# Triangular inverses for two head pairs at once, decays by one masked scan, and a new order of the mixers' parts

## The chip, the cores and the metric

The kernel runs on one core of one Trainium2 chip. The metric is the device time of one execution in microseconds; the time before is the median of three runs. The core has TensorE (matrix products, written to PSUM), VectorE, ScalarE and GpSimd (POOL) for elementwise work, and SyncE (SP), which here only issues transfers; ScalarE and POOL issue some too. Each engine takes its instructions in the order in which the program holds them.

## What is computed

The reference is one layer of a hybrid decoder on 512 tokens of width 1024, in float32: RMS norm, one wide input projection, four token mixers of width 512, gates that merge them, then a gated feed-forward part with a short convolution, a gated per-layer input, and a last norm.

```python
h = rmsnorm(x, norm_mix); proj = h @ w_in
xa, xb, xc, xd, g = split(proj)
branches = (pool_mixer(xa), rwkv7_mixer(xb), spatial_gating_mixer(xc), hgrn2_mixer(xd))
merged = sum(sigmoid(g[k]) * (branches[k] @ w_branch[k]) for k in range(4))
x = x + merged @ w_out
x = x + conv_glu_ffn(rmsnorm(x, norm_ffn))
x = x + (p @ ple_proj) * sigmoid(rmsnorm(x, norm_ple) @ ple_gate)
return rmsnorm(x, norm_final)
```

The change is in the second mixer. It has 8 heads of width 64 and a state that is decayed and corrected at every token:

```python
w = -softplus(-(w0 + tanh(lw) @ w2)) - 0.5;  decay = exp(-exp(w))
sa = einsum('bhvk,bhk->bhv', state, -kk_t)
state = state * w_t + sa[..., None] * (kk_t * a_t) + v_t[..., None] * k_t
y_t = einsum('bhvk,bhk->bhv', state, r_t)
```

## The kernel before

Activations lie with channels on the 128 partitions and the 512 tokens along the free axis, eight tiles for the width of 1024. A float32 product is made of three faster ones: each operand is split into a rounded part hi and a remainder lo (`split`, L76: a cast on ScalarE, L77, and a difference on VectorE or POOL, L78), and `mm3` (L118) issues hi*hi, hi*lo and lo*hi (L119 to L121). A weight block of 128 x 1024 (512 KB) is loaded by SP into one of two raw buffers and split into a ring of four (NWS) hi and four lo tiles, tags wh and wl; a block of 256 output columns and eight input tiles takes two places in each ring. The gemms write into four PSUM banks (`mm_ps`), all other products into four more (`sm_ps`).

The second mixer works on four head pairs j, each two heads of 64 channels, and on eight chunks of 64 tokens:

- `rwkv_proj` (task x): three projections r, k, v of a pair. `rwkv_decay` (w): decay and step size; the sigmoid and an Exp give the decay per token (L382 to L385).
- `rwkv_prep` (prep): E, the running product of the decays inside each chunk, by eight scans on VectorE (L399); the normed key kk; its head sums by a product with a block mask (pk, pb); 1/E by a reciprocal (L422); the factors ard, BK and BD; and v turned (pv into M).
- `rwkv_forms` (forms): products of these per chunk (pg, L471), masked into AR (L475), and written to DRAM, from which the strictly triangular 32 x 32 blocks come back into U with one block on each of 32 partitions.
- `rwkv_inverse` (inv): 30 steps of elimination on U, two VectorE instructions each (L496, L498), a write to DRAM, and eight block loads into two zeroed tiles TB, issued by ScalarE's and SP's queues. Then the off-diagonal blocks: transposes Ts (L518), products pW (L521) and pT (L527) with evictions, and copies on ScalarE that refill AR (L534) once pW has read it.
- `rwkv_chain` (chain j.half): eight dependent steps per pair, each three products (cx, cu, cs) with small evictions between (L550, L554, L563).
- `rwkv_finish` (fin) reads the outputs, norms them, and stores them; `rwkv_out` brings all four back.

The other tasks are the pool (pool), the spatial gating (sgp, sgv, sgn, sgu), the gated recurrence (masks, hv, hg, head, ho), and per branch and column block `gates` (gate) and `merge`. A gate's sigmoid (L880) goes straight from PSUM on ScalarE; the branch product is multiplied into it on VectorE.

The order is written out by hand in ORDER: the tasks are emitted as they stand there, those with "!" with an earlier due time. A planner then orders each engine's instructions when the program is built, by due time among those that its own cost model says are ready; on the chip each engine keeps to that order. Buffers of one tag are a ring: a tile that has no free place makes its first writer wait.

After the mixers come the output projection, the feed-forward part (its activated tiles, tag act, in 44 places) and the ple stage, in which four gate weights (wpg) pass through the same ring of split weights.

Of the kernel before, what the change touches and what calls it, by code (L numbers as in the profile page):

```python
# [16 lines left out]
P = 128  # L17
# [13 lines left out]
NR, NF, NWR, NWS, NA = 22, 7, 2, 4, 4  # L31
# [17 lines left out]
def hybrid_kernel(ctx, tc, x, p, norm_mix, w_in, pool_w, pool_scale, rwkv_mu, rwkv_w0, rwkv_w2, rwkv_a0,  # L49
# [65 lines left out]
    def wcols(w, c0, name, early=True):  # L115
        return wload(w[:, c0:c0 + WB].rearrange("(k p) c -> p k c", p=P), KD, WB, name, early)
# [160 lines left out]
    zer = cp.tile([P, C], F32, name="zer")  # L277
    G.memset(zer, 0.0)
# [15 lines left out]
    low, oml, noml = lbs[:, 3], lbs[:, 4], lbs[:, 5]  # L294

# [77 lines left out]
    def rwkv_decay(j):  # L373
        assert "lora" in ready
        pt = sm_ps(f"pw{j}")
        pa = sm_ps(f"pa{j}")
        js = slice(j * P, (j + 1) * P)
        for i, o in enumerate((pt, pa)):
            PE.matmul(o, lwa[i][:, js], mwa[i], start=True, stop=False)
            PE.matmul(o, lwa[i][LH[i], js], mlo[LH[i], :], start=False, stop=True)  # L380
        wd = rt(f"wd{j}")
        S.activation(wd, pt, AF.Sigmoid, bias=ctab["w0"][:, j:j + 1])  # L382
        a = rt(f"a{j}")
        S.activation(a, pa, AF.Sigmoid, bias=ctab["a0"][:, j:j + 1])
        S.activation(wd, wd, AF.Exp, scale=-math.exp(-0.5))  # L385
        rw[j].update(wd=wd, a=a)
# [6 lines left out]
    def rwkv_prep(j):  # L393
        js = slice(j, j + 1)
        r, k, v, wd, a = (rw[j].pop(n) for n in (0, 1, 2, "wd", "a"))
        E = rt(f"E{j}")
        for c in range(NCH):
            cs = slice(c * C, (c + 1) * C)
            V.tensor_tensor_scan(E[:, cs], wd[:, cs], zer, 1.0, ALU.mult, ALU.add)  # L399
# [21 lines left out]
        Em = nr  # L421
        V.reciprocal(Em, E)  # L422
# [37 lines left out]
    def rwkv_forms(j):  # L460
# [23 lines left out]
        U = rg.tile([32, 32, 32], F32, tag="U", name=f"U{j}")  # L484
        sf = scr1.rearrange("(f s) (c g t) -> f c s g t", f=2, g=2, t=32)
        for f in range(2):
            (nc.scalar, nc.sync)[f].dma_start(U[f * 16:(f + 1) * 16], sf[f, :, :, f, :])
        rw[j].update(AR=AR, BKe=BKe, U=U)

    def rwkv_inverse(j):  # L490
        U, AR, ard = (rw[j][n] for n in ("U", "AR", "ard"))
        tmp = rg.tile([32, 16 * 16], F32, tag="Ut", name=f"Ut{j}")
# [8 lines left out]
        scr2 = dp.tile([32, 1024], F32, tag="scr2", name=f"scr2_{j}")  # L501
        nc.scalar.dma_start(scr2, Uf)
        s2 = scr2.rearrange("(f i c h) (s t) -> f i h s c t", f=2, i=2, h=2, s=32)
# [3 lines left out]
        Ts = Ws = rg.tile([P, 2, HC, 32], F32, tag="Ts", name=f"Ts{j}")  # L507
        for i in range(2):
            G.memset(TB[i], 0.0)
            for h in range(2):  # L510
                for f in range(2):
                    (nc.scalar, nc.sync)[f].dma_start(TB[i][(lo, hi)[f][h], :, h, f * 32:f * 32 + 32], s2[f, i, h])

        blocks = lambda q: q[:, :T // 2].rearrange("p (i c x) -> p i c x", i=2, c=HC)
        pw, pt = ([blocks(sm_ps(f"p{n}{j}_{h}")) for h in range(2)] for n in "WT")
        for h in range(2):
            for i in range(2):
                V.transpose(Ts[lo[h], i], TB[i][lo[h], :, h, 0:32])  # L518
                for c in range(HC):
                    q = i * HC + c  # L520
                    PE.matmul(pw[h][hi[h], i, c, :], AR[q // 2][lo[h], q % 2, 0, h, 32:C], Ts[lo[h], i, c, :],  # L521
                              start=True, stop=True, tile_position=(lo[h].start, hi[h].start))
            V.tensor_copy(Ws[hi[h]], pw[h][hi[h]])
        for h in range(2):
            for i in range(2):
                for c in range(HC):
                    PE.matmul(pt[h][lo[h], i, c, :], Ws[hi[h], i, c, :], TB[i][hi[h], c, h, 32:],  # L527
                              start=True, stop=True, tile_position=(hi[h].start, lo[h].start))
                V.tensor_copy(TB[i][lo[h], :, h, 32:], pt[h][lo[h], i])

        for q in range(4):
            cs = slice(q % 2 * 2, q % 2 * 2 + 2)
            for h in range(2):
                S.copy(AR[q][hr(h), :, 0, h, :], ard[q // 2][hr(h), cs, 0:C])  # L534
        rw[j]["TB"] = TB

    def rwkv_chain(j, half):
        AR, BKe, M, TB, dec = (rw[j][n] for n in ("AR", "BKe", "M", "TB", "dec"))

# [3 lines left out]
        for c in range(half * HC, half * HC + HC):  # L543
# [83 lines left out]
    def pool_group(gb):  # L627
        if not pl:
# [3 lines left out]
            for i in range(16):  # L632
                G.memset(pl["inv"][:, i:i + 1], 1.0 / (i + 1))
# [443 lines left out]
    for nb in range(4):  # L1077
        wpg[nb] = wcols(ple_gate, nb * WB, f"pg{nb}")
# [49 lines left out]
```

## Time and profile before

| | us |
|---|---|
| median of three runs | 1193.68 (1193.16 to 1193.85) |
| profiled execution | 1199.85 |
| its span, first to last instruction | 1198.1 |
| TensorE busy in the span | 1127.5 (94%) |
| VectorE, ScalarE, POOL busy | 778.0, 469.7, 223.2 |
| mean granted TensorE clock | 0.970 |

The rows below come from the profiled execution and are timed from its first instruction. PE is TensorE's matmuls, PEld its weight loads (which overlap them), DVE is VectorE, ACT ScalarE; "q" behind a name is the engine's own queue, from which transfers are issued. L with a number is a line of the kernel before. In a timeline a row gives start, duration, engine, line, operation, out<-in by the program's names, and in brackets how long the engine stood idle before it and what ended that. In a list of lines it is: group, count, busy time in all and mean in ns, then idle time ahead of it and what ended most of it. PEclk is the granted clock as a share of full speed.

### The profile page before, as it was taken

The page shows a single profiled execution, that of the slowest core. Times are in us where ns is not written, and L with a number is a line of the kernel's source. Part 1 is how long each engine was busy: PE and PEld are TensorE (multiplying, and loading weights), DVE is VectorE, ACT ScalarE, POOL GpSimd, SP SyncE. Part 2 cuts the span into 40 slices and gives each one's busy share as a digit, 9 for nine tenths or more (in the row PEclk, how much of TensorE's full clock was granted, in tenths as well). Part 3 has the DMA queues.
Part 4 walks back from the last instruction along what each step waited for, and adds up shares of the span by engine and source line. Part 5 has one row for each costly group of instructions (what it writes and reads, how often), then busy time and mean ns, then how long its engine had stood idle before and what let it go on. Part 6 is the DMA issues. An engine that isn't in the chain of part 4 may idle for free. (4 is left out here: it accounts for less than half of the span.)

```text
span 1198.1 us, 15929 instructions
## 1 busy us (share of the span) xinstructions
PE 1127.5 (94%) x5978; PEld 916.5 (76%) x5978; DVE 778.0 (65%) x1438; ACT 469.7 (39%) x720; POOL 223.2 (19%) x256
## 2 busy tenths in 40 slices
PE   7999999999698996599999999999999999999997
PEld 5777667877487774468777788888888888888897
DVE  5688878884778587545666466567766776333345
ACT  5633632554242331323213454444444444222262
POOL 7020120000221030000132114312221322111101
PEclk9999999999699998699999999999999999999999
DMA  8422332222133222014211135233233322233521
GB/s 278 131 79 64 95 89 71 54 89 74 43 83 90 77 60 77 19 53 123 79 38 53 52 104 161 83 93 106 82 95 106 105 89 88 97 97 97 167 89 71
DMA packets 121388, 107.86 MB, mean 90 GB/s; under 512 B 17628, under 2 KB 115678, under 8 KB 121312
## 3 DMA queue, kind: packets, MB, share of 16 engines
q1 hardware_dynamic: 104860, 94.74, 26.0%
q10 hardware_dynamic: 15364, 9.97, 2.9%
q0 software_dynamic: 1088, 2.14, 0.6%
q8 instruction: 47, 0.77, 0.3%
q14 instruction: 29, 0.24, 0.1%
HBM read 100.01 MB, written 6.82 MB: 89 GB/s over the span
## 5 line engine op out<-in xcount | busy, mean ns | idle before, releaser
L119 PE MATMUL pgate<-hT,wh_g 128*128 128x512 f32 x256 | 104.6, 409 | 4.4 <-ACT gt L880 3.5
L120 PE MATMUL pgate<-hT,wh_g 128*128 128x512 f32 x256 | 104.4, 408 | 0.0
L121 PE MATMUL pgate<-hT,wl_g 128*128 128x512 f32 x256 | 104.4, 408 | 0.0
L119 PE MATMUL pfd<-act_h,wh_fd 128*128 128x512 f32 x176 | 69.3, 394 | 0.0
L121 PE MATMUL pfd<-act_h,wl_fd 128*128 128x512 f32 x176 | 69.0, 392 | 0.0
L120 PE MATMUL pfv<-x1n,wh_fv 128*128 128x512 f32 x176 | 68.6, 390 | 0.0
L121 PE MATMUL pfv<-x1n,wl_fv 128*128 128x512 f32 x176 | 68.6, 390 | 0.0
L119 PE MATMUL pfv<-x1n,wh_fv 128*128 128x512 f32 x176 | 68.6, 390 | 0.0
L120 PE MATMUL pfg<-x1n,wh_fg 128*128 128x512 f32 x176 | 68.5, 389 | 0.0
L119 PE MATMUL pfg<-x1n,wh_fg 128*128 128x512 f32 x176 | 68.5, 389 | 0.0
L121 PE MATMUL pfg<-x1n,wl_fg 128*128 128x512 f32 x176 | 68.5, 389 | 0.0
L120 PE MATMUL pfd<-act_l,wh_fd 128*128 128x512 f32 x176 | 68.3, 388 | 0.0
L78 DVE TENSOR_TENSOR wl_fd<-wr_fd,wh_fd 128x1024 fp32r<-128x1024 f32 (+1 forms) x24 | 29.1, 1214 | 57.0 <-ACT wh_fd L77 57.0
L119 PEld LDWEIGHTS pgate<-hT,wh_g 128*128 128x128 f32 x256 | 49.3, 193 | 14.3 <-ACT gt L880 3.9
L1022 POOL TENSOR_TENSOR cv<-cv,cg 128x512 f32<-128x512 f32 x22 | 28.4, 1290 | 169.9 <-DVE cv L1000 169.9
L77 ACT CAST wh_g<-wr_g 128x1024 fp32r<-128x1024 f32 x32 | 33.6, 1049 | 60.4 <-PE pgate L120 19.0
L120 PEld LDWEIGHTS pgate<-hT,wh_g 128*128 128x128 f32 x256 | 49.4, 193 | 9.2 <-issue 0.2
L121 PEld LDWEIGHTS pgate<-hT,wl_g 128*128 128x128 f32 x256 | 49.1, 192 | 9.3 <-issue 0.2
L120 PE MATMUL pbr<-bol,wh_br 128*128 128x512 f32 x128 | 52.1, 407 | 0.0
L119 PE MATMUL pbr<-boh,wh_br 128*128 128x512 f32 x128 | 51.5, 403 | 0.0
L121 PE MATMUL pbr<-boh,wl_br 128*128 128x512 f32 x128 | 51.4, 401 | 0.0
L78 DVE TENSOR_TENSOR wl_g<-wr_g,wh_g 128x1024 fp32r<-128x1024 f32 x32 | 41.3, 1290 | 10.0 <-ACT wh_g L77 9.7
(451 smaller groups left out, 3039.3 us busy)
## 6 DMA issues: line engine op xcount, KB each, us to landing
wr_g<-in_w_in_dram SPq DMA_DIRECT2D x32, 512.0 KB, 3.7
wr_fg<-in_ffn_up_dram SPq DMA_DIRECT2D x22, 512.0 KB, 3.5
wr_fv<-in_ffn_up_dram SPq DMA_DIRECT2D x22, 512.0 KB, 3.5
wr_fd<-in_ffn_down_dram SPq DMA_DIRECT2D x20, 512.0 KB, 3.5
wr_br<-in_w_branch_dram SPq DMA_DIRECT2D x16, 512.0 KB, 3.6
wr_rkv<-in_w_in_dram SPq DMA_DIRECT2D x12, 512.0 KB, 3.9
wr_wo<-in_w_out_dram SPq DMA_DIRECT2D x8, 512.0 KB, 4.6
wr_pg<-in_ple_gate_dram SPq DMA_DIRECT2D x8, 512.0 KB, 3.6
```

Source lines behind the costliest of these rows:

```text
L77: S.copy(hi, src)
L78: lo_eng.tensor_tensor(lo, src, hi.bitcast(F32), ALU.subtract)
L119: PE.matmul(o, l[0], r[0], start=first, stop=False)
L120: PE.matmul(o, l[0], r[1], start=False, stop=False)
L121: PE.matmul(o, l[1], r[0], start=False, stop=last)
L1022: G.tensor_tensor(c, c, cg[i], ALU.mult)
```

## The change

Two head pairs share one U tile of 64 partitions and one `rwkv_inverse`: the elimination runs once for pairs 0 and 1 and once for 2 and 3. The four tiles TB are fixed, zeroed once, and used by both inverses. The products pW and pT are issued with the two heads alternating, and their evictions, as those of the chain, go one to VectorE and one to ScalarE. In the decay, the sigmoid alone is kept; one scan over 512 columns with a pattern of ones that is zero at the head of each chunk sums it, and two Exps give E and 1/E. The ring of split weights has three places, the last two ple gate weights are split into the ring act, the ring r has 23 places instead of 22, and ORDER is new. Some assertions on the order, which issue nothing, are left out below.

```diff
-NR, NF, NWR, NWS, NA = 22, 7, 2, 4, 4
+NR, NF, NWR, NWS, NA = 23, 7, 2, 3, 4
...
-!masks lora x.0.2 w.0 x.0.0 x.0.1 !prep.0 !forms.0 x.1.1 pool.0 x.1.2 !pool.1 !sgp x.2.0 !x.1.0 w.1 !merge.0.0
-merge.0.3 !prep.1 !forms.1 !inv.0 !x.3.2 !chain.0.0 x.2.1 !chain.0.1 w.2 merge.0.1 fin.0 !x.2.2 inv.1
-!chain.1.0 !cols hv.1 !sgv.0 !w.3 sgv.1 !chain.1.1 prep.2 !fin.1 merge.0.2 !forms.2 !x.3.1 sgn !sgu.1 sgu.0
-!gate.3.0 merge.2.1 inv.2 !chain.2.0 x.3.0 !merge.2.0 !prep.3 forms.3 !chain.2.1 !gate.3.3 merge.2.2 inv.3
-hg.1 !fin.2 merge.2.3 gate.3.2 !hg.0 !chain.3.0 !chain.3.1 fin.3 !out hv.0 !head.0 !head.3 !head.2 ho.3
-merge.1.1 !head.1 ho.2 ho.0 merge.1.2 merge.1.0 merge.1.3 ho.1 gate.3.1 merge.3.0 !merge.3.2 merge.3.1
+!x.0.1 lora w.0 !x.0.2 x.0.0 prep.0 !masks x.1.2 x.1.1 w.1 !x.1.0 !prep.1 !forms.0 pool.0 pool.1 forms.1
+x.2.2 merge.0.2 !merge.0.0 merge.0.3 !sgp !sgv.1 sgv.0 !inv.0 merge.0.1 !chain.0.0 !chain.1.0 !chain.1.1
+chain.0.1 fin.0 !sgn !x.3.2 fin.1 x.2.0 sgu.1 sgu.0 x.2.1 x.3.0 x.3.1 !w.3 gate.3.3 !w.2 !prep.2 !forms.2
+prep.3 !forms.3 !inv.1 !cols merge.2.1 merge.2.2 merge.2.0 !chain.3.0 !merge.2.3 !hg.1 !chain.2.0
+!chain.2.1 gate.3.0 fin.2 !chain.3.1 !fin.3 out hv.0 hv.1 hg.0 merge.1.1 !head.2 head.3 ho.3 merge.1.3
+!ho.2 merge.1.2 !head.1 merge.1.0 !head.0 ho.0 ho.1 gate.3.1 merge.3.1 merge.3.0 !gate.3.2 merge.3.2
 merge.3.3
...
-    def wload(src, a, b, name, early=True):
+    def wload(src, a, b, name, early=True, ring=None):
...
+                if ring:
+                    for q in range(0, kn, T // b):
+                        hi, lo = (ring(f"{tg}_{name}{k0 + q}").rearrange("p (a b) -> p a b", b=b)
+                                  for tg in ("wh", "wl"))
+                        split(raw[:, q:q + T // b, :], hi, lo)
+                        res += [(hi[:, k, :], lo[:, k, :]) for k in range(T // b)]
+                    continue
...
-    zer = cp.tile([P, C], F32, name="zer")
-    G.memset(zer, 0.0)
+    rst = cp.tile([P, T], F32, name="rst")
+    G.memset(rst, 1.0)
+    cst_ = G.memset(rst.rearrange("p (c s) -> p c s", c=NCH)[:, :, 0:1], 0.0)
...
+    TBs = [rg.tile([P, T], F32, tag=f"TB{i}", name=f"TB{i}") for i in range(4)]
+    with tc.issue_after(cst_.ins):
+        for t in TBs:
+            G.memset(t, 0.0)
...
-        S.activation(wd, wd, AF.Exp, scale=-math.exp(-0.5))
...
-        E = rt(f"E{j}")
-        for c in range(NCH):
-            cs = slice(c * C, (c + 1) * C)
-            V.tensor_tensor_scan(E[:, cs], wd[:, cs], zer, 1.0, ALU.mult, ALU.add)
+        E, Em = rt(f"E{j}"), wd
+        V.tensor_tensor_scan(E, rst, wd, 0.0, ALU.mult, ALU.add)
+        S.activation(Em, E, AF.Exp, scale=math.exp(-0.5))
+        S.activation(E, E, AF.Exp, scale=-math.exp(-0.5))
...
-        Em = nr
-        V.reciprocal(Em, E)
...
-        U = rg.tile([32, 32, 32], F32, tag="U", name=f"U{j}")
+        if j % 2 == 0:
+            rw[j]["U"] = rg.tile([2 * 32, 32, 32], F32, tag="U", name=f"U{j}")
+        U = rw[j]["U"] = rw[j - j % 2]["U"]
+        u0 = j % 2 * 32
...
-    def rwkv_inverse(j):
+    def rwkv_inverse(jj):
+        js = (2 * jj, 2 * jj + 1)
+        U = rw[js[0]]["U"]
+        tmp = rg.tile([2 * 32, 16 * 16], F32, tag="Ut", name=f"Ut{jj}")
...
-            V.tensor_tensor(tv, U[:, 0:s, s:s + 1].broadcast_to([32, s, n]),
-                            U[:, s:s + 1, s + 1:].broadcast_to([32, s, n]), ALU.mult)
+            V.tensor_tensor(tv, U[:, 0:s, s:s + 1].broadcast_to([2 * 32, s, n]),
+                            U[:, s:s + 1, s + 1:].broadcast_to([2 * 32, s, n]), ALU.mult)
...
-        TB = [c4(rt(f"TB{j}_{i}")) for i in range(2)]
...
-            G.memset(TB[i], 0.0)
+        for q, j in enumerate(js):
+            TB = rw[j]["TB"] = [c4(t) for t in TBs[2 * q:2 * q + 2]]
+            for i in range(2):
+                for h in range(2):
+                    for f in range(2):
+                        (nc.scalar, nc.sync)[f].dma_start(TB[i][(lo, hi)[f][h], :, h, f * 32:f * 32 + 32],
+                                                          s2[q, f, i, h])
...
+        for j in js:
...
+            for h in range(2):
+                (V.tensor_copy, S.copy)[h](Ws[hi[h]], pw[h][hi[h]])
...
+            for h in range(2):
+                for i in range(2):
+                    (V.tensor_copy, S.copy)[h](TB[i][lo[h], :, h, 32:], pt[h][lo[h], i])
...
             for h in range(2):
-                V.tensor_copy(X[hr(h)], px[hr(h), hr(h)])
+                (V.tensor_copy, S.copy)[h](X[hr(h)], px[hr(h), hr(h)])
...
             for h in range(2):
-                V.tensor_copy(m[hr(h), h, :], pu[hr(h)])
+                (V.tensor_copy, S.copy)[h](m[hr(h), h, :], pu[hr(h)])
...
-        wpg[nb] = wcols(ple_gate, nb * WB, f"pg{nb}")
+        wpg[nb] = wcols(ple_gate, nb * WB, f"pg{nb}", ring=at if nb > 1 else None)
```

## Rows read from the trace of the kernel before

**Rows 1.** Stretches: length, busy (count) of PE, PEld, DVE, ACT, POOL; PEclk, DMA, GB/s.
```profile
27.40:305.50 278.10, 269.96 (x1481) 212.35 (x1481) 218.35 (x500) 127.87 (x209) 26.11 (x29) 0.99 0.30 84
305.50:333.00 27.50, 15.97 (x135) 12.23 (x136) 20.38 (x47) 6.49 (x15) 5.77 (x9) 0.63 0.16 39
333.00:468.20 135.20, 128.54 (x625) 100.92 (x624) 103.10 (x214) 45.47 (x78) 25.28 (x22) 0.96 0.27 76
468.20:502.40 34.20, 11.12 (x133) 9.12 (x134) 24.07 (x79) 8.54 (x18) 0.00 (x0) 0.55 0.15 40
502.40:692.00 189.60, 184.03 (x1097) 147.01 (x1097) 109.77 (x230) 57.58 (x86) 34.25 (x41) 1.00 0.23 68
692.00:1130.00 438.00, 437.95 (x1961) 361.61 (x1960) 253.14 (x276) 179.41 (x228) 100.64 (x73) 1.00 0.33 104
```

**Rows 2.** TensorE's waits, 30 to 720 us: total, times, longest.
```profile
PE pW L521 <- DVE Ts L518: 22.1, 2, 21.3
PE pb L367 <- ACT hs0b L77: 8.1, 4, 6.6
```

**Rows 3.** Timeline of TensorE about the second hole.
```profile
467.75 0.39 PE L121 MATMUL phf<-hT,wl_hgf 128*128 128x512 f32 x1
489.46 1.56 PE L521 MATMUL pW<-Ts,AR 32*32 32x32 f32 x24 [21.32 <-DVE Ts L518]
```

**Rows 4.** Timeline of VectorE: fourth inverse, first and last step, first transpose.
```profile
460.90 0.18 DVE L496 TENSOR_TENSOR Ut<-U 32x30 f32<-32x30 f32 x1
...
484.91 0.20 DVE L498 TENSOR_TENSOR U<-U,Ut 32x30 f32<-32x30 f32 x1
489.01 0.30 DVE L518 STREAM_TRANSPOSE Ts<-TB 32x128 f32<-32x128 f32 x1 [3.90 <-DMA TB<-scr]
```

**Rows 5.** Timeline of ScalarE in the first and the second hole.
```profile
311.40 0.62 ACT L77 CAST hs0b<-kk 128x512 fp32r<-128x512 f32 x1 [7.32 <-DVE kk L425]
...
487.15 1.81 ACTq L512 DMA_DIRECT2D TB<-scr  x4
489.89 1.56 ACT L534 COPY AR<-ard 64x128 f32<-64x128 f32 x6 [20.85 <-PE pW L521]
...
495.74 0.60 ACT L770 ACTIVATE hq<-phq 128x512 f32<-128x512 f32 x1
```

**Rows 6.** The stretch of the first inverse, columns as in rows 1.
```profile
95.90:146.70 50.80, 48.65 (x199) 36.67 (x198) 46.50 (x120) 24.45 (x31) 3.77 (x4) 0.97 0.29 89
```

**Rows 7.** Groups by line on VectorE, whole span.
```profile
L496 DVE TENSOR_TENSOR Ut<-U 32x30 f32<-32x30 f32 (+14 forms) x120 | 42.1, 351 | 3.3
L498 DVE TENSOR_TENSOR U<-U,Ut 32x30 f32<-32x30 f32 (+14 forms) x120 | 40.5, 337 | 3.1
...
L550 DVE COPY X<-cx 64x64 f32<-64x64 f32 x64 | 14.2, 222 | 8.5 <-PE cx L547 7.3
...
L422 DVE RECIPROCAL nr<-E 128x512 f32<-128x512 f32 x4 | 13.4, 3341 | 0.0
L399 DVE TENSOR_TENSOR_SCAN E<-wd,zer 128x64 f32<-128x64 f32 x32 | 6.6, 272 | 0.1
```

**Rows 8.** Timeline of VectorE: products on 128 and on 64 partitions.
```profile
155.08 0.41 DVE L420 TENSOR_TENSOR ard<-xb,E 128x256 f32<-128x256 f32 x1
...
163.34 0.41 DVE L436 TENSOR_TENSOR BK<-a,nr 64x256 f32<-64x256 f32 x1
```

**Rows 9.** Groups by line on ScalarE and POOL, whole span.
```profile
L385 ACT ACT_TABLE_LOAD x4 | 5.1, 1283 | 0.1
...
L567 ACT COPY ard<-M 64x64 f32<-64x64 f32 x56 | 13.6, 242 | 36.5 <-DVE M L563 30.2 <-DVE M L566 4.5
...
L509 POOL MEMSET TB<- 128x512 f32 x8 | 4.2, 527 | 84.1 <-ACT xb L315 51.5 <-PE cs L558 14.7 <-DVE Ys L607 8.1
```

**Rows 10.** Timeline in the feed-forward part: a weight's cast and another's difference.
```profile
873.85 1.06 ACT L77 CAST wh_fg<-wr_fg 128x1024 fp32r<-128x1024 f32 x1 [0.95 <-PE pfg L120]
...
885.82 2.12 DVE L78 TENSOR_TENSOR wl_fv<-wr_fv,wh_fv 128x1024 fp32r<-128x1024 f32 x1 [0.40 <-ACT wh_fv L77]
```

More of the change, by code (lines that the diff above doesn't have):

```diff
@@ L113, in wload, with wcols @@
         return res
-    def wcols(w, c0, name, early=True):
-        return wload(w[:, c0:c0 + WB].rearrange("(k p) c -> p k c", p=P), KD, WB, name, early)
+    def wcols(w, c0, name, early=True, ring=None):
+        return wload(w[:, c0:c0 + WB].rearrange("(k p) c -> p k c", p=P), KD, WB, name, early, ring)
     def mm3(o, l, r, first, last):
@@ L500, in rwkv_inverse @@
         V.memset(Uf[:, 0:1024:33], 1.0)
[L501 removed]
+        scr2 = dp.tile([2 * 32, 1024], F32, tag="scr2", name=f"scr2_{jj}")
         nc.scalar.dma_start(scr2, Uf)
[L503 to L505 removed]
+        s2 = scr2.rearrange("(j f i c h) (s t) -> j f i h s c t", j=2, f=2, i=2, h=2, s=32)
         lo, hi = [slice(h * C, h * C + 32) for h in range(2)], [slice(h * C + 32, h * C + C) for h in range(2)]
[L507 removed]
@@ L517, in rwkv_inverse @@
+        blocks = lambda q: q[:, :T // 2].rearrange("p (i c x) -> p i c x", i=2, c=HC)
+        for j in js:
+            AR, TB, ard = (rw[j][n] for n in ("AR", "TB", "ard"))
+            Ts = Ws = rg.tile([P, 2, HC, 32], F32, tag="Ts", name=f"Ts{j}")
+            pw, pt = ([blocks(sm_ps(f"p{n}{j}_{h}")) for h in range(2)] for n in "WT")
+            for h in range(2):
+                for i in range(2):
+                    V.transpose(Ts[lo[h], i], TB[i][lo[h], :, h, 0:32])
             for i in range(2):
-                V.transpose(Ts[lo[h], i], TB[i][lo[h], :, h, 0:32])
@@ L519, in rwkv_inverse @@
                 for c in range(HC):
                     q = i * HC + c
[L521 to L524, printed above, removed]
+                    for h in range(2):
+                        PE.matmul(pw[h][hi[h], i, c, :], AR[q // 2][lo[h], q % 2, 0, h, 32:C], Ts[lo[h], i, c, :],
+                                  start=True, stop=True, tile_position=(lo[h].start, hi[h].start))
@@ L525, in rwkv_inverse @@
+            for h in range(2):
+                (V.tensor_copy, S.copy)[h](Ws[hi[h]], pw[h][hi[h]])
             for i in range(2):
                 for c in range(HC):
[L527 to L532, printed above, removed]
-            for h in range(2):
-                S.copy(AR[q][hr(h), :, 0, h, :], ard[q // 2][hr(h), cs, 0:C])
@@ L535, in rwkv_inverse @@
-        rw[j]["TB"] = TB
+                    for h in range(2):
+                        PE.matmul(pt[h][lo[h], i, c, :], Ws[hi[h], i, c, :], TB[i][hi[h], c, h, 32:],
+                                  start=True, stop=True, tile_position=(hi[h].start, lo[h].start))
+            for h in range(2):
+                for i in range(2):
+                    (V.tensor_copy, S.copy)[h](TB[i][lo[h], :, h, 32:], pt[h][lo[h], i])
+            for q in range(4):
+                cs = slice(q % 2 * 2, q % 2 * 2 + 2)
+                for h in range(2):
+                    S.copy(AR[q][hr(h), :, 0, h, :], ard[q // 2][hr(h), cs, 0:C])
@@ L537, in rwkv_chain @@
     def rwkv_chain(j, half):
         AR, BKe, M, TB, dec = (rw[j][n] for n in ("AR", "BKe", "M", "TB", "dec"))
+        assert rw[j].setdefault("half", 0) == half
+        rw[j]["half"] += 1
         SS = [a[:, :, 0:C] for a in rw[j]["ard"]]
@@ L588, in rwkv_finish @@
         js = slice(j, j + 1)
+        assert rw[j]["half"] == 2
         rwkv_read(j)
@@ L631, in pool_group @@
             pl["inv"] = rg.tile([P, 16], F32, tag="inv", name="inv")
-            for i in range(16):
-                G.memset(pl["inv"][:, i:i + 1], 1.0 / (i + 1))
+            with tc.issue_after(cst_.ins):
+                for i in range(16):
+                    G.memset(pl["inv"][:, i:i + 1], 1.0 / (i + 1))
         pw, inv = pl["w"], pl["inv"]
@@ L702, in sg_v @@
             gelu_to(vs[t][:, vb * WB:(vb + 1) * WB], pt, WB, f"v{vb}_{t}")
+        sgd[f"v{vb}"] = True
     def sg_norm():
         vs = sgd["vs"]
+        assert sgd.pop("v0") and sgd.pop("v1")
+        sgd["normed"] = True
         mv = rg.tile([P, NT, 2], F32, tag="sgmv", name="sgmv")
```

23 lines of the change are left out of this document (10 added, 13 removed).

## The prediction

> **What bounds the kernel now.** I read the stretches first, because the share of busy time over the whole span averages stages with different limits. From 692 to 1130 us TensorE is busy 437.95 of 438.0 us at full clock [rows 1]: the feed-forward part runs at the rate of its matmuls, 438.0/1961 = 0.223 us each, and nothing in this change makes it shorter. From 27.4 to 692 us, the four mixers and the merges, TensorE is idle 8.1 + 11.5 + 6.7 + 23.1 + 5.6 = 55 us. Two of the stretches stand out, 305.5 to 333.0 and 468.2 to 502.4, with granted clocks of 0.63 and 0.55. The granted clock has two levels, 2.4 GHz and half of it, 1.2, so a mean of 0.63 is half rate for 74% of the stretch and 0.55 for 90%.
>
> What each costs: hole 1 (27.5 us, 15.97 busy) loses 11.5 idle and, at most, half of the busy time at half rate, 8.0; together 19.5. Hole 2 (34.2 us, 11.12 busy) loses 23.1 + 5.6 = 28.7. Sum 48.2. Elsewhere in the mixers 20.4 us are idle, and half rate (0.01 and 0.04 missing of 278 and 135 us, so 5.6 + 10.8 us at half rate) loses 8.2. With all of it gone the profiled execution of 1199.9 us (span 1198.1) would stand at 1123; that is the floor.
>
> Next the waits say what ends the holes: TensorE waits 21.3 us for the transposes Ts behind an inverse, and 6.6 us once for pb [rows 2]. The three engines' orders in hole 2 then show the mechanism. TensorE's last q/f matmul starts at 467.75 and the next, pW of the fourth inverse, at 489.46 [rows 3]. VectorE does that inverse from 460.90 to 485.1, and the first transpose runs at 489.01, 3.9 us behind its DMA [rows 4]. ScalarE has the copies into AR (L534) at the head of its queue and waits 20.85 us for pW; the sigmoids that would empty the four gemm banks (hq, hk) stand behind it and run from 495.74 on [rows 5]. So TensorE had other work but no free bank for it, and its next instruction was pW anyway. This needs a late inverse and a full set of banks at once: the first inverse lasted 50.8 us and TensorE was busy in 48.65 of them [rows 6].
>
> **The change, part by part.** *Pair inverses.* 240 VectorE instructions (42.1 + 40.5 us) become 120 of the same free size on 64 instead of 32 partitions [rows 7]. Whether twice the partitions cost time no row of this form shows. Bounds: -41.3 us of VectorE (no cost) to 0 (double cost). I take -41.3, for the nearest rows are two products of 256 elements, one on 64 and one on 128 partitions, of 0.41 us each [rows 8]. Behind a pair stand 16 block loads instead of 8: four took 1.81 us on ScalarE's queue [rows 5], so +1.8 us on each queue, SP's too, where weight loads stand behind them. The two heads share one Ts tile, so the second waits for the first: 0 to 5 us per pair, of which I take nothing, since the first head's chain starts meanwhile.
>
> *Decays.* Per head eight scans (0.272 each, 6.6 us in all) become one of 512 columns: between 0.82 us (twice a product of 256 columns, 0.41 [rows 8]) and 2.18 (eight times); I take 1.1, near the product, a gain of 2.2 us over four heads, bounds -2.1 and +3.3. The reciprocal of E goes, 13.4 us [rows 7]. One more Exp comes on ScalarE per head, 4 x 0.60 = 2.4 us, as an estimate from a sigmoid of its size [rows 5]. The Exps move behind the scan, next to the square root.
>
> Where this meets the tables: a change of function set costs ScalarE 1283 ns, four times at the old place of the Exp [rows 9]. The Exps stay together, so I count no more loads; the bounds are none and two more per head, 10.3 us of ScalarE. The Trainium skill's page "ScalarE: Activation LUTs", section "Rules for kernel authors", says to budget about 2.7 us for every switch and to finish one set first; by it the two loads per head would be 21.6 us, by the row 10.3, and I go by the row.
>
> *Copies split between the engines.* Half of L550 and of its twin L554 (64 copies and 14.2 us each) goes to ScalarE, at 242 ns by its own copies of that size against 222 [rows 7, 9]: 14.2 us off VectorE, 15.5 on ScalarE. In the chain each pair of copies gets about 0.2 us shorter, 32 x 2 x 0.2 = 13 us of latency over four heads, at nothing for the time where gate or merge matmuls lie beside the chain. Queued behind them on ScalarE are the weight casts, which have 2 us to spare (below). If ScalarE stands blocked, the same copies lengthen the chain (rival C).
>
> VectorE thus loses 41.3 + 13.4 + 2.2 + 14.2 = 71 us of work, all of it in the mixers; ScalarE, which is busy half as long there [rows 1], gets 18 more.
>
> *Fixed tiles.* The eight memsets on POOL wait 84.1 us in all for buffers, 51.5 once [rows 9]; four at the start replace them, with one of the reset pattern, 5 x 0.53 = 2.6 us of POOL behind its startup work: 0 to 2.6. I take 0.
>
> *The ring of split weights, 4 to 3, and its other tile for the last two gate weights.* The second half of a weight can now be cast only when the first half of the weight before is done with, 24 matmuls x 0.223 = 5.4 us ahead of use instead of 10.7 or more. It needs a cast of 1.06 and a difference of up to 2.12 [rows 10], 3.3 with handovers: 2 us to spare. I take 0; the upper bound is rival D, and below nothing I have none, for TensorE is never idle there. The split pieces of the last two ple weights no longer wait in this ring: 0 to -3 us at the tail, taken as 0.
>
> *The new order.* Pair 0 and pair 1 each run prep, forms, inverse, chains and finish; pair 1 must wait for pair 0's ard and block tiles. Beside the second inverse stand gate and merge matmuls of branch 2, whose evictions (sigmoids) need ScalarE alone: four banks x 24 x 0.223 = 21.4 us of matmuls, against 28.1 us from 460.90 to 489.01. SP's weight loads and POOL's adds move with their parts.
>
> The sum, on the profiled execution: hole 2 goes, -28.7; hole 1 goes by half, -9.7 (of the 7.32 us that ScalarE waited there for kk [rows 5], the reciprocal of 3.34 that goes is about half); half rate elsewhere by half, -4.1; and one of the two pair inverses leaves half a hole 2, +14.4, between 0 and two whole ones. Total -28.1: 1171.8. The profiled execution lies 6.2 us above the median of 1193.7; the same offset gives **1166 us**, with 1150 to 1184 as this case's own range.
>
> **The rivals.** *B, everything covered.* Both inverses lie under matmuls and hole 1 closes: -28.7 - 19.5 - 4.1 = -52.3, 1141 us. For it: the first inverse [rows 6], and the lighter VectorE. Against it: 20.4 us of other idle time in an order that has the same engines.
>
> *C, slower: ScalarE blocked at both inverses.* The copies into AR wait for pW in each, now 16 of them, and with them the chain's new copies and the banks' sigmoids. Price per pair: 28.7 + 1.8 (loads) + 8 x 0.26 (copies) = 32.6; two 65.2, with half of hole 1 left 74.9 instead of 48.2: +26.7, 1220 us. It turns slower when the two together exceed 38.5, 19 us each. Against it: one of four inverses did so before. The trace shows ScalarE's queue kept its order through 20.85 us [rows 5]. The Trainium skill's page "TensorE: Matmul & The Clock Gate", section "Architectural detail: the array is 16x 32x32, not 1x 128x128", says that the queues of ScalarE and VectorE are strictly first in, first out; by that rule every copy moved to ScalarE is one more that such a wait holds, and the trace agrees.
>
> *D, the short ring.* If the weights' second halves come 1 us late in each of 22 up-projections, 12 pieces of the down-projection and 4 of the output: +38, 1204 us. It needs 3 us of other work in front of the difference on VectorE, more than the difference itself takes.
>
> *E, the holes only move.* VectorE's relief falls where TensorE was busy, and new places wait as long: 1193 us. Against it: the largest wait is an inverse, and half of the inverses' instructions are gone.
>
> **How the numbers follow.** Forecast 0.50, B 0.20, C 0.12, D 0.08, E 0.10. Half a microsecond in 1193 is noise in the three runs; 0.2%, about 2.4 us, is what such a measurement can tell from no change. Faster: 0.50 + 0.20 + 0.03 of E = 0.73; same: 0.05 of E; slower: 0.12 + 0.08 + 0.02 of E = 0.22. The range of 1134 to 1206 reaches over B and D and leaves out most of C and the last stretch to the floor, about 0.18.
>
> **What would show it.** Right: the inverse's two lines at 120 instructions and about 41 us; no wait of TensorE of over 15 us for Ts; VectorE busy some 70 us less; TensorE idle in the mixers by 25 to 35 us instead of 55; still no idle time in the feed-forward part. Wrong: inverse steps twice as long; ScalarE's AR copies again waiting 20 us; TensorE waiting for wl of ffn weights; or a clock under 0.7 in some new stretch.

## The result, and the profile after

The changed kernel takes **1147.43 us** (median of four runs, 1145.79 to 1150.41) against 1193.49 (1193.16 to 1193.85) beside it: ratio 0.9617, 95% interval 0.9597 to 0.9637. The forecast was 1166: faster was right, but 19 us too little, below the 1150 to 1184 given for the likeliest case and inside the whole range of 1134 to 1206. The profiled execution took 1145.79 us, 54.1 less than that of before. The medians lie 46.1 apart, for the profiled run of before lay 6.2 us above its median and this one lies 1.6 below.

Where it came from is read as before, stretches first. The stretches end at the two pair inverses (150.9 to 195.7 and 380.5 to 421.5), the last read-out matmul cy of the second mixer (497.5), the start of the output projection (675.5), and, as the last row, the feed-forward stretch that answers to the last of [rows 1]. Columns as there.

```profile
28.00:150.90 122.90, 113.98 (x516) 88.48 (x517) 91.75 (x149) 59.52 (x89) 18.98 (x20) 0.97 0.30 83
150.90:195.70 44.80, 43.94 (x296) 37.16 (x295) 35.06 (x88) 13.94 (x25) 0.52 (x1) 1.00 0.32 89
195.70:380.50 184.80, 180.47 (x1065) 142.53 (x1064) 123.11 (x247) 96.33 (x191) 30.66 (x28) 1.00 0.29 81
380.50:421.50 41.00, 39.92 (x223) 31.04 (x222) 32.57 (x79) 9.89 (x18) 4.03 (x3) 1.00 0.36 93
421.50:497.50 76.00, 73.87 (x596) 61.20 (x594) 39.56 (x113) 39.21 (x106) 1.30 (x1) 1.00 0.27 81
497.50:675.50 178.00, 174.21 (x961) 138.77 (x956) 107.54 (x191) 55.57 (x74) 43.49 (x46) 1.00 0.24 73
675.50:1144.10 468.60, 460.75 (x2249) 388.20 (x2247) 264.34 (x322) 192.08 (x272) 97.44 (x74) 1.00 0.32 101
...
638.70:1076.70 438.00, 437.90 (x1947) 361.23 (x1946) 249.90 (x270) 174.59 (x223) 99.75 (x71) 1.00 0.34 104
```

The reader is to see that no stretch like the two holes is left: TensorE is busy for 43.94 of 44.8 us and 39.92 of 41.0 us of the two pair inverses, at the full clock, where the stretch of hole 2 had 11.12 of 34.2 at 0.55. Behind 675.5 nothing changed (468.6 us; before 469.3). So nearly all of it lies in the mixers. TensorE's longest waits there, which answer to [rows 2] (total, times, longest), are now small, and none is for the transposes behind an inverse:

```profile
PE pb L384 <- ACT hs0b L77: 5.5, 3, 2.6
PE plo L685 <- DVE plm L683: 4.3, 2, 3.3
PE ph L874 <- DVE hQ L870: 1.4, 2, 0.8
PE cu L581 <- ACT X L579: 1.2, 2, 0.6
```

Against [rows 3], where 21.3 us of nothing stand ahead of pW, TensorE's timeline behind the second pair inverse shows pW between matmuls of another mixer:

```profile
415.76 0.39 PE L130 MATMUL phf<-hT,wl_hgf 128*128 128x512 f32 x1
416.15 0.41 PE L546 MATMUL pW<-Ts,AR 32*32 32x32 f32 x8
416.48 0.50 PE L128 MATMUL phf<-hT,wh_hgf 128*128 128x512 f32 x1
```

The groups on VectorE that answer to [rows 7]:

```profile
L518 DVE TENSOR_TENSOR U<-U,Ut 64x30 f32<-64x30 f32 (+14 forms) x60 | 21.3, 355 | 1.8
L516 DVE TENSOR_TENSOR Ut<-U 64x30 f32<-64x30 f32 (+14 forms) x60 | 19.3, 322 | 4.9 <-DMA U<-scr 3.3
...
L579 DVE COPY X<-cx 64x64 f32<-64x64 f32 x32 | 6.9, 215 | 12.1 <-PE cx L576 11.9
L414 DVE TENSOR_TENSOR_SCAN E<-rst,wd 128x512 f32<-128x512 f32 x4 | 4.9, 1218 | 0.4 <-ACT wd L399 0.4
```

The elimination is half as many instructions of the same mean: 64 partitions cost what 32 did. And on ScalarE, answering to [rows 5] and [rows 9], the block loads and the copies into AR, behind which TensorE is no longer kept waiting:

```profile
412.03 5.44 ACTq L531 DMA_DIRECT2D TB<-scr  x8
417.51 0.92 ACT L562 COPY AR<-ard 64x128 f32<-64x128 f32 x3 [6.17 <-PE pW L546]
...
422.12 0.60 ACT L815 ACTIVATE hk<-phf 128x512 f32<-128x512 f32 x1
```

**An account that holds for all the kernels.** Each profiled span is 28 us of start, the time in the mixers up to the output projection, and what lies behind. I took TensorE's idle time in the mixers, and what half rate cost there (busy time times what the clock lacks of 1), summed over stretches of 10 us. What is left, TensorE's work at full rate, comes out nearly the same for all, 623 to 630 us and 619 in e8, so most of what sets the kernels apart stands in the two columns ahead of it:

| kernel | median | span | idle | half rate | work at full rate | behind |
|---|---|---|---|---|---|---|
| before | 1193.5 | 1198.1 | 55.0 | 19.1 | 626.7 | 469.3 |
| changed | 1147.4 | 1144.1 | 21.1 | 3.4 | 623.0 | 468.6 |
| e1, new order, old work | 1209.0 | 1207.0 | 47.2 | 33.5 | 630.0 | 468.3 |
| e2, old order, new work | 1190.3 | 1188.7 | 41.5 | 26.3 | 623.5 | 469.4 |
| e3, two eliminations | 1183.3 | 1180.8 | 39.1 | 22.2 | 623.0 | 468.5 |
| e4, old decays | 1161.0 | 1157.9 | 29.0 | 7.5 | 625.1 | 468.3 |
| e5, copies on VectorE | 1157.5 | 1158.1 | 24.4 | 11.0 | 626.1 | 468.6 |
| e6, before with AR copies on POOL | 1197.0 | 1191.9 | 53.7 | 14.3 | 626.5 | 469.4 |
| e7, one gate put later | 1157.4 | 1152.5 | 25.8 | 6.6 | 623.3 | 468.8 |
| e8, norm by a power on POOL | 1472.4 | 1469.9 | 343.2 | 10.5 | 619.3 | 468.9 |
| e9, BK on VectorE | 1153.4 | 1151.4 | 23.0 | 5.3 | 626.2 | 468.9 |
| e10, norm by Ln and Exp | 1158.7 | 1158.3 | 26.3 | 12.3 | 623.0 | 468.7 |
| e11, both | 1148.1 | 1149.9 | 19.7 | 8.3 | 625.6 | 468.3 |
| e12, pb later | 1144.7 | 1143.5 | 17.1 | 4.7 | 625.1 | 468.6 |

Of the 54.0 us of span, 33.9 are idle time, 15.7 half rate, 3.7 work and 0.7 the tail. Every experiment is read by these two columns: what moved, and where. A few us in them are the single execution's: e6, in the order of before, has 14.3 us at half rate, 4.8 less than the profiled execution of before, which lay 6.2 us above its median. The gain is the 46.1 of the medians.

### The profile page after: what moved, and what is told of

Read it like the earlier page. It is cut to its first block, busy times and chain, and to the rows that moved or that the text cites. A ratio compares the mean times of both kernels' runs of the same rounds, so it can differ in the third digit from the quotient of the medians.

```text
span 1144.1 us, 15616 instructions
## 1 busy us (share of the span) xinstructions
PE 1107.0 (97%) x5978; PEld 902.6 (79%) x5978; DVE 709.4 (62%) x1212; ACT 480.9 (42%) x798; POOL 221.9 (19%) x253
## 4 chain that ended last, share of the span: by engine, by line
PE 84%; DVE 8%; ACT 3%; issue 2%; DMA 2%; POOL 0%; SPq 0%; POOLq 0%; ACTq 0%; DVEq 0%
PE pgate L130 4%; PE pgate L129 4%; PE pgate L128 4%; PE pfd L128 4%; PE pfv L128 3%; PE pfv L129 3%; PE pfg L129 3%; PE pfg L128 3%; PE pfg L130 3%; PE pfv L130 3%; PE pfd L130 3%; PE pfd L129 3%; PE pbr L129 2%; PE pbr L130 2%; PE pbr L128 2%
## 5 line engine op out<-in xcount | busy, mean ns | idle before, releaser
L128 PE MATMUL pgate<-hT,wh_g 128*128 128x512 f32 x256 | 102.6, 401 | 0.0
L129 PE MATMUL pgate<-hT,wh_g 128*128 128x512 f32 x256 | 101.0, 395 | 0.0
L129 PE MATMUL pfv<-x1n,wh_fv 128*128 128x512 f32 x176 | 68.6, 390 | 0.0
L130 PE MATMUL pfv<-x1n,wl_fv 128*128 128x512 f32 x176 | 68.6, 390 | 0.0
L128 PE MATMUL pfv<-x1n,wh_fv 128*128 128x512 f32 x176 | 68.6, 390 | 0.0
L1059 POOL TENSOR_TENSOR cv<-cv,cg 128x512 f32<-128x512 f32 x22 | 28.4, 1290 | 170.0 <-DVE cv L1037 170.0
L129 PEld LDWEIGHTS pgate<-hT,wh_g 128*128 128x128 f32 x256 | 48.2, 188 | 9.2 <-issue 0.2
L128 PEld LDWEIGHTS pgate<-hT,wh_g 128*128 128x128 f32 x256 | 48.2, 188 | 9.1 <-issue 0.5
L77 ACT CAST wh_fd<-wr_fd 128x1024 fp32r<-128x1024 f32 (+1 forms) x24 | 23.6, 982 | 58.5 <-PE pfd L129 55.8
```

Of the source, the lines that this page charges most:

```text
L77: S.copy(hi, src)
L128: PE.matmul(o, l[0], r[0], start=first, stop=False)
L129: PE.matmul(o, l[0], r[1], start=False, stop=False)
L130: PE.matmul(o, l[1], r[0], start=False, stop=last)
L1059: G.tensor_tensor(c, c, cg[i], ALU.mult)
```

## The experiments

**e1 and e2: the order and the work apart.** e1 keeps the new order, fixed tiles and ring, and puts back all of VectorE's work: the diffs of e3, e4 and e5 together. e2 keeps the new code and takes the order of before, as far as pairs allow:

```diff
-... !prep.1 !forms.1 !inv.0 !x.3.2 !chain.0.0 x.2.1 !chain.0.1 w.2 merge.0.1 fin.0 !x.2.2 inv.1 !chain.1.0 ...
+... !prep.1 !forms.1 !inv.0 !x.3.2 !chain.0.0 x.2.1 !chain.0.1 w.2 merge.0.1 fin.0 !x.2.2 !chain.1.0 ...
-... merge.2.1 inv.2 !chain.2.0 x.3.0 !merge.2.0 !prep.3 forms.3 !chain.2.1 !gate.3.3 merge.2.2 inv.3 ...
+... merge.2.1 x.3.0 !merge.2.0 !prep.3 forms.3 !gate.3.3 merge.2.2 inv.1 !chain.2.0 !chain.2.1 ...
```

> The changed kernel (1147.4 us) with its order, fixed tiles and ring kept, but VectorE's work put back: the elimination of a pair done one head after the other on 32 partitions (240 instructions, about 41 us more), eight scans with a reciprocal per head (about 15 us more), all copies of chain and inverse on VectorE (about 14 us more). Theory O (the order closes the holes: gate and merge matmuls with free banks stand beside both inverses, so VectorE's length hardly matters): 1147 to 1160. Theory V (the gain is VectorE's 69 us of work that went): 1175 to 1195, with TensorE waiting 15 to 20 us for the block transposes behind each pair. If both are needed: 1160 to 1175.

> The changed kernel with the parts in the order of before, as far as pairs allow: the first pair's inverse where the first inverse stood (behind both heads' forms), the second pair's where the fourth stood, with head 2's two chain halves moved behind it. Pair inverses, new decays, split copies, fixed tiles and ring stay. Theory O: hole 2 comes back, because the second pair's inverse stands as late as the fourth did with four full gemm banks before it: 1175 to 1193, and TensorE waits 15 us or more behind that inverse. Theory V: the lighter VectorE closes the holes in any order: 1147 to 1160.

Measured: e1 1208.97 (ratio to before 1.0135, 1.012 to 1.015), e2 1190.34 (0.9972, 0.9959 to 0.9986). Theory O, that the order does it, failed in e1: alone it is 16 us slower than before, above every range written down for it, theory V's and the mixed one too. Theory V, that the lighter VectorE does it, failed in e2: alone it is worth 3 us there. e2's order is not quite that of before, for head pair 2's chains had to move behind the pair inverse. Its time lies in theory O's range, but not for O's reason: hole 2 did not come back, and TensorE's longest wait for Ts is 5.3 us, at the first inverse:

```profile
210.35 1.50 PE L545 MATMUL pW<-Ts,AR 32*32 32x32 f32 x24 [5.31 <-DVE Ts L540]
```

Together the two halves are worth 46. The longest of the stretches where time is lost, first in e1 (new order, old work), then in e2:

```profile
440.00:530.00 90.00, 73.03 (x419) 60.64 (x418) 50.22 (x137) 22.45 (x52) 1.42 (x1) 0.73 0.23 65
```

```profile
205.00:255.00 50.00, 30.41 (x240) 22.30 (x240) 12.63 (x50) 15.89 (x59) 0.00 (x0) 0.53 0.06 11
```

In e1 it is the end of the second pair's elimination, its pW, pT and chains, in e2 the first pair's pW, pT and chains: 17.0 us idle and 0.27 x 73 = 20 at half rate in the one, 19.6 and 0.47 x 30.4 = 14 in the other. In e2 VectorE is busy for 12.6 of these 50 us, ScalarE for 15.9, and the DMA engines for 0.06 of it: nothing is overloaded. TensorE's groups there are almost only the chain's own small products, each with a short wait:

```profile
L575 PE MATMUL cx<-M,AR 128*128 128x128 f32 x16 | 6.2, 488 | 5.3 <-DVE M L591 4.7 <-DVE M L594 0.7
L586 PE MATMUL cs<-M,BKe 128*128 128x128 f32 x14 | 5.6, 501 | 3.8 <-ACT M L582 3.8
L580 PE MATMUL cu<-X,TB 128*128 128x64 f32 x16 | 5.5, 447 | 3.8 <-ACT X L578 3.8
```

Such a chain, with no other matmul beside it, has short waits by the dozen, the granted clock falls to near its lower level (0.53 in the mean), and its products then take 488 ns in the mean (cx; 297 in the changed kernel).

**e3, e4, e5: one part undone at a time** in the changed kernel.

```diff
-        for s in range(1, 31):            # 64 partitions
+        for o in (0, 32):                 # e3: 32 partitions, one head pair after the other
+            u, tm = U[o:o + 32], tmp[o:o + 32]
+            for s in range(1, 31):
...
-        V.tensor_tensor_scan(E, rst, wd, 0.0, ALU.mult, ALU.add)   # e4: as before
+            V.tensor_tensor_scan(E[:, cs], wd[:, cs], zer, 1.0, ALU.mult, ALU.add)
...
+        V.reciprocal(Em, E)
...
-                (V.tensor_copy, S.copy)[h](X[hr(h)], px[hr(h), hr(h)])   # e5, and the three others
+                V.tensor_copy(X[hr(h)], px[hr(h), hr(h)])
```

> The changed kernel with one thing undone: the elimination of a pair runs on 32 partitions for one head and then for the other, 240 instructions instead of 120, each of the two inverses about 20 us longer. Theory O: nothing, 1146 to 1152, for other matmuls stand beside the inverse. Theory V: each inverse shows with its 20 us, 1180 to 1188.

> The changed kernel with the decays of before: per head eight scans of 64 columns, one Exp, and the reciprocal of 512 columns on VectorE (3.34 us). Theory O: within 2 us of 1147.4. Theory V: VectorE's 15 us more show in the waits for pb and kk in front of the forms: 1155 to 1163. The tables: by the count of the changed kernel (33 loads of 1283 ns against 39) six loads come back on ScalarE, 7.7 us there.

> The changed kernel (1147.4) with one thing undone: the copies of chain and inverse stand all on VectorE again, two one after the other instead of one on each engine. Theory P (after four runs: the mixers end a fixed 645 to 648 us behind the last read-out matmul cy, and that one is the end of the path prep, forms, inverse, chain of the second pair; what VectorE takes longer on it shows at 0.85 to 0.95 of its length): the chain pairs get 0.2 us longer each, 32 copies in the second pair's chains, which run interleaved, so 3 to 7 us on the path of that pair and some of the first pair's: 1152 to 1159; the order alone with all of VectorE's work back lost 61.6, of which the eliminations are 35.9 and the decays 13.5, and 12 are left for these. Rival: the copies lie under gate and merge matmuls and show nothing, 1146 to 1149.

Measured: 1183.34 (ratio to before 0.9931, 0.9906 to 0.9957), 1160.98 (0.9733, 0.9707 to 0.9760) and 1157.53 (0.9703, 0.9686 to 0.9719). Against the changed kernel these are +35.9, +13.6 and +10.1, together 59.6; e1, with all three, has 61.5. The first two lie in theory V's ranges, the third in theory P's. In the new order VectorE's work thus counts nearly in full, as theory V has it: the eliminations are 41.4 us longer here (82.0 in two groups against 40.6). The price is not paid at the inverse. TensorE's wait for Ts in e3 is 1.9 us. The stretch from there over pW, pT and most of the chains pays the largest part, 11.1 us idle and 0.17 x 68.9 = 11.7 at half rate; the changed kernel has 2.1 and none from 421.5 to 497.5. The rest is spread over the mixers:

```profile
L520 DVE TENSOR_TENSOR U<-U,Ut 32x30 f32<-32x30 f32 (+14 forms) x120 | 41.0, 342 | 3.0
L518 DVE TENSOR_TENSOR Ut<-U 32x30 f32<-32x30 f32 (+14 forms) x120 | 41.0, 341 | 3.0
```

```profile
430.00:510.00 80.00, 68.92 (x442) 55.30 (x442) 35.66 (x101) 28.53 (x84) 1.31 (x1) 0.83 0.23 67
```

The longer inverse is covered by gate matmuls which are then missing beside the chains: in the changed kernel 48 of them run there (425 to 498 us), in e3 16 (460 to 536). So the last cy comes later, and what lies behind it stays. The last read-out group of the changed kernel and of e3 (count, shortest/median/longest ns, first and last start):

```profile
L610 PE MATMUL cy<-M,AR x128: 222/222/270, 260.2 to 497.5; 128*64 128x64 f32 x128
```

```profile
L612 PE MATMUL cy<-M,AR x128: 221/222/270, 272.2 to 535.6; 128*64 128x64 f32 x128
```

From there to the end it is 646.6 and 645.2 us; in e1 647.9, in e4 645.0. In e4 the table loads stayed 33, against what I expected, and e1 has 33 too: the old decays bring none back in this order.

**e6: hole 2 of the kernel before.** The prediction had put it down to ScalarE's queue, held by the copies into AR. Here POOL does them.

```diff
-                S.copy(AR[q][hr(h), :, 0, h, :], ard[q // 2][hr(h), cs, 0:C])
+                G.tensor_copy(AR[q][hr(h), :, 0, h, :], ard[q // 2][hr(h), cs, 0:C])
```

> The kernel before (1193.5) with one thing changed: the eight copies into AR behind each inverse go to POOL, so that ScalarE's queue no longer stands behind pW and its sigmoids empty the four gemm banks. Theory of the prediction (ScalarE's blocked queue makes hole 2): hole 2 closes by half or more, 1178 to 1186. Theory P (the fourth inverse comes late on the path, and matmuls run beside it are missing later beside the chain): hole 2 gets shorter but the last cy stays near 562 and the time within 3 us: 1191 to 1197.

Measured: 1196.97 (1.003, 1.0014 to 1.0045). The time lies where theory P had it, but the hole did not get shorter: it stayed whole, and another copy, which needs TensorE's cy from behind pW, stood at ScalarE's head. Rows of TensorE and of ScalarE:

```profile
483.45 1.37 PE L521 MATMUL pW<-Ts,AR 32*32 32x32 f32 x24 [21.55 <-DVE Ts L518]
```

```profile
489.28 0.37 ACT L585 COPY Ys<-cy 128x256 f32<-128x256 f32 x1 [26.47 <-PE cy L581]
```

The copies into AR were a sign and not the cause. TensorE's own queue has pW next, so it waits for Ts whatever ScalarE does. That ScalarE's queue has no part in it is not shown: the banks' sigmoids stood behind the other copy (hq at 489.55), so the four banks stayed full here too, and no run of this order had them free.

**e7: the cover itself.** No work is added or taken; one gate's 48 matmuls go from beside the second pair's chains to behind the last read-out.

```diff
-!chain.2.1 gate.3.0 fin.2 !chain.3.1 !fin.3 out hv.0 hv.1 hg.0 ... ho.0 ho.1 gate.3.1 ...
+!chain.2.1 fin.2 !chain.3.1 !fin.3 out hv.0 hv.1 hg.0 ... ho.0 ho.1 gate.3.0 gate.3.1 ...
```

> The changed kernel with one gate (gate.3.0, 48 matmuls of 512 columns, 48 x 0.223 = 10.7 us of TensorE) taken from beside the second pair's inverse and chains and put behind the last read-out. No engine has more or less work. Theory P: the last cy stays at about 497 and the chain stands barer: 1153 to 1160. Rival (TensorE's own work alone bounds the changed kernel): the last cy comes 10 us earlier and the time stays, 1146 to 1149.

Measured: 1157.43, +10.0 us, for 10.7 us of matmuls. The last cy starts at 496.2 (497.5 in the changed kernel) and 656.3 us lie behind it instead of 646.6. As theory P has it, the bare place is in the chains: 6.5 us idle and 0.15 x 28.5 = 4.3 at half rate, against 1.6 and none in the same stretch of the changed kernel, the second row.

```profile
440.00:475.00 35.00, 28.48 (x227) 24.95 (x226) 13.93 (x55) 13.63 (x46) 0.00 (x0) 0.85 0.11 31
440.00:475.00 35.00, 33.40 (x285) 29.75 (x284) 16.12 (x49) 16.04 (x51) 0.00 (x0) 1.00 0.26 77
```

**e8 to e12: can it be faster?** If the path through VectorE and TensorE's work are both at their limit, a shorter path gives little. e9 moves the BK products of the second head to VectorE; e10 replaces the norm of kk and leaves out its floor of 1e-12; e11 is both; e8 has e9 and another norm; e12 moves the head sum pb, for which TensorE waits longest, to the end of the prep.

```diff
-            for h, eng in enumerate((V, G)):        # e9, e8, e11
+            for h, eng in enumerate((V, V)):
...
-        S.activation(nr, pk, AF.Sqrt)               # e10, e11; e8 below
-        V.tensor_scalar(nr, nr, 1e-12, None, ALU.max)
-        V.reciprocal(nr, nr)
+        S.activation(nr, pk, AF.Ln)
+        S.activation(nr, nr, AF.Exp, scale=-0.5)
...
+        V.tensor_scalar(nr, pk, 1e-24, None, ALU.max)
+        G.tensor_tensor(nr, nr, epst[:, 3:4].broadcast_to([P, T]), ALU.pow)
...
-        pb = sm_ps(f"pb{j}")                       # e12: these lines stand behind M
-        head_sum(pb, rkp, f"b{j}")
-        bv = rt(f"bv{j}")
-        V.tensor_tensor(bv, pb, v, ALU.mult)
```

> The changed kernel with a shorter path in the preps: the norm's square root on ScalarE and its reciprocal on VectorE (3.35 us each) become one maximum on VectorE and one power on POOL, and the BK products of the second head go from POOL (1.15 and 0.90 us each) to VectorE (0.41). VectorE loses 4 x 3.35 us and gains 16 x 0.41 = 6.6. Theory P: the path gets shorter, but TensorE is idle for only some 13 us in the mixers behind the first 60 us, so the gain is between 2 and 8 us: 1139 to 1145. Rival (TensorE bounds it all now, its waits are not on this path): 1146 to 1149. A power of 512 columns on POOL has not been seen in a trace here; if it takes over 5 us, it is slower: 1150 or more.

> The changed kernel with one thing more: the BK products of the second head run on VectorE (0.41 us each) instead of POOL (1.15 and 0.90). Four products of a head took 4.1 us on POOL beside VectorE's own four (1.6); all eight on VectorE take 3.3. Theory P (the path through the preps, inverses and chains stands at its limit together with TensorE): the path gets about 0.8 us per head shorter, 0 to 3 us in all: 1144 to 1148. Rival (VectorE's own load counts, and it gets 6.6 us more): 1149 to 1154.

> The changed kernel with the norm of kk as Ln and Exp on ScalarE in place of square root, maximum and VectorE's reciprocal (0.79 and 3.35 us per head, 16.6 in all). The trace has no Ln; its price is taken as a sigmoid's 0.60 and one table load of 1.28. Theory P: the path gets about 4 us per head shorter, but TensorE is idle only some 13 us in the mixers behind the first 60 us: the time falls by 2 to 8 us, 1139 to 1145, and no further. If VectorE's length alone set the time at 0.85 of its work, as the four runs that put work back showed, it would fall by 14: 1133. If TensorE alone bounds it: 1146 to 1149.

> Both changes of the two runs before together. Theory P: little more than the better of the two, 1138 to 1145, with TensorE's idle time in the mixers down from 21 to some 15 us, most of what is left in the first 60 us. Rival: the two gains add.

> The changed kernel with TensorE's own wait moved: the head sum pb and its product bv, which only the finish needs, stand at the end of each prep instead of ahead of BK, BD and M. TensorE waits 6.0 us in all for the casts of pb in the changed kernel. Account (start 28 us, 623 to 630 us of TensorE's work at full rate in the mixers, its idle time and what half rate costs, 469 us behind): of the idle 21.1 us some 5 go, 1142 to 1145. Rival, after the two runs in which small reliefs made the kernel slower by 6 and 11 us: the rebuilt order of the instructions moves other matmuls too, and that outweighs it, 1148 to 1158.

Measured: e8 1472.39, by one group on POOL (below), for which the last sentence on e8 had left room; e9 1153.36 (ratio 0.9672, 0.9649 to 0.9695), e10 1158.68 (0.9702, 0.9684 to 0.9721), e11 1148.06 (0.9619, 0.9597 to 0.9641), e12 1144.72 (0.9585, 0.9562 to 0.9607).

```profile
L424 POOL TENSOR_TENSOR nr<-nr,epst 128x512 f32<-128x512 f32 x4 | 329.7, 82430 | 0.0
```

e9 and e10 were to lighten the path and are 6 and 11 us slower than the changed kernel; together, in e11, they are as fast as it, against both of e11's expectations. e9 lies in the range of its rival, that VectorE's own load counts (6.6 us more): its last cy starts 8.6 us later, and what lies behind it stays, 645.3 us.

```profile
L610 PE MATMUL cy<-M,AR x128: 222/222/270, 260.9 to 506.1; 128*64 128x64 f32 x128
```

e10 lies in no range that was written down. TensorE waits 11.7 us for the casts of pb there, 5.5 in the changed kernel. The last cy starts at 499.4, but 658.9 us lie behind it: the planner, whose costs see the new instructions, had put 66 matmuls more behind it (1027 against 961 up to the output projection).

```profile
499.40:689.60 190.20, 187.03 (x1027) 149.66 (x1022) 111.12 (x195) 58.18 (x78) 44.59 (x46) 1.00 0.25 75
```

That sets a limit to the single differences above: every kernel's order of instructions was rebuilt, and by e10 such a rebuilding may move the time by about 10 us. e1, e3 and the gap between e2 and the changed kernel are well beyond that. e4 and e5 are not, so their 14 and 10 us are not settled one by one. e7's size is not either, but its last cy and its bare place say where it lies. e12 has 4.0 us less idle time, near the 5 that the account gave, and is 2.7 us below the changed kernel by the medians; the intervals of the two ratios overlap, so it is the fastest version seen and not shown to be faster. None of the five is, and whether a shorter path would gain anything stays open.

## Why the prediction was right, and where not

*The limit.* Right: TensorE's idle time and its half rate in the mixers were nearly the whole of it (49.6 of 54.0 us), and the feed-forward part did not move. Idle time was forecast at 25 to 35 us and is 21.1; half rate in hole 1, hole 2 and elsewhere fell from 19.1 to 3.4.

*Hole 2, -28.7.* Right that it goes. Its cause was half right: the rows show a late inverse with nothing else ahead of its pW in TensorE's queue, and e6 shows that the copies into AR are not needed for the hole. What the full banks add is not shown.

*The step that failed: "one of the two pair inverses leaves half a hole 2, +14.4".* This term was mis-sized. Its bounds were 0 and two holes, and it measured next to nothing: 0.9 us idle beside the first pair inverse and 1.1 beside the second, at the full clock. The row that speaks for that was there: [rows 6], the first inverse, covered in 48.65 of 50.8 us. Of the inverses in the rows one was covered and one bare, and I charged half a bare one to the new order without working out what would stand beside its second pair: gate, q, f and merge matmuls up to the moment of pW, as its timeline shows.

*Hole 1 by half, -9.7.* It went whole, 19.5 by the forecast's own price. I had argued from the reciprocal alone. The 27.5 us that begin 6.6 us ahead of the third pair's pb, the place of hole 1, are these in the changed kernel, in e1 and in e2:

```profile
323.30:350.80 27.50, 25.37 (x131) 19.88 (x130) 21.93 (x34) 13.67 (x22) 12.77 (x12) 1.00 0.43 110
352.50:380.00 27.50, 26.24 (x136) 20.60 (x135) 24.88 (x48) 12.07 (x20) 11.11 (x11) 1.00 0.30 80
316.70:344.20 27.50, 24.46 (x184) 19.17 (x184) 17.30 (x44) 11.31 (x20) 1.71 (x4) 0.94 0.38 101
```

Before, TensorE was busy for 15.97 of them at 0.63 [rows 1]. Either half of the change closes this hole alone (the work in e2 all but 4.5 us); the order, which does it in e1 with the reciprocal back, I had not priced. With these two terms right, -28.7 - 19.5 - 4.1 = -52.3 (rival B), against 54.0 less in the span. That is partly luck: of idle time and half rate, which make up the 52.3, 49.6 went, and the other 4.4 are work and tail that no term named.

*The offset.* The forecast took 6.2 us off for the profiled execution's place above the median. That of the changed kernel lies 1.6 below its own. Measured by medians, the saving is 46.1, so B's 1141 would have missed by 6 us on the other side.

*VectorE's 71 us.* The amount was right (778.0 to 709.4, 68.6), and so were its parts: eliminations 40.6 us (forecast 41.3), scans 1.22 us each (1.1), Exps 0.63 (0.60). But the sum gave the decays only a share of hole 1 and the copies nothing. By e3, e4 and e5 eliminations, decays and copies are worth 36, 14 and 10 us in the new order (the last two with the reserve above), and e1 agrees with their sum, 61.5; by e2 all of them are worth 3 in the order nearest to the old one. The terms are not a sum: the order decides whether a shorter path is worth anything, and the shorter path whether the order has matmuls enough for its chains. ScalarE got 11.2 us more instead of 18, since six table loads went (39 to 33, 1283 ns each: 7.7 us), by the order, as e1 and e4 have 33 too.

On the loads the Trainium skill's page "ScalarE: Activation LUTs", section "Table sets: the hidden batching unit", says that Ln followed by Exp needs one load, as one set holds both. e10's rows disagree: the Exp right behind the Ln (L424) had a load of its own, four times. Which set each load brought, no row shows.

```profile
L423 ACT ACT_TABLE_LOAD x4 | 5.1, 1283 | 0.1
L424 ACT ACT_TABLE_LOAD x4 | 5.1, 1283 | 0.1
```

*The rivals.* C (ScalarE blocked at both inverses) did not come: its AR copies wait at most 6.17 us, with the block loads at 5.44 us on its queue, not the 3.6 that I had counted. D (the short ring) did not: 437.90 of 438.0 us busy. E (the holes only move) is what both halves of the change do when made alone, in e1 (even 16 us slower) and e2.

## What to carry to other kernels

When a serial path runs beside work that fills the gaps, the work is a stock, as e3 and e7 show here: matmuls used to cover a long inverse are missing beside the chain that follows, so the time is lost where TensorE is bare and not where the long instruction stands. Count the stock over the whole path before pricing a relief, and price an order and a relief together, in both orders. Where a queue stands blocked, move the blocked instruction in an experiment before calling it the cause.

## What the runs showed of the hardware

- A power of 128x512 float32 elements on POOL took 82.4 us; a product of that size takes 1.3 to 1.8 us there (L1059 1290 ns, L438 1806).
- 64 partitions cost VectorE no more than 32 in the elimination: 322 and 355 ns in the mean against 341 and 342 in e3.
- A scan of 512 columns took 1218 ns, against 272 for 64 columns [rows 7]. Short ones overlap (32 of them kept VectorE busy for 6.6 us, not 8.7), so eight cost 1.35 times one long one (6.6 against 4.9 us for four heads).
